# Attention weights: two of the eight diagonal chunks of a head turned by transfers, with products of their own for the last 128 columns

## The chip, the cores and the metric

The kernel runs on one core of one Trainium2 chip. The metric is the device time of one execution in microseconds, taken as the median over several executions; a profile of one execution shows where the time is spent. The engines are TensorE (PE in the profile, its weight loads PEld), VectorE (DVE), ScalarE (ACT), GpSimd (POOL) and SyncE (SP), whose queue issues nearly all transfers.

## The reference, cut to what matters

The program is a two-layer decoder trunk over 1024 positions with width 1024: a recurrent layer with a feed-forward network, then a stick-breaking attention layer with 16 heads of 64 dimensions and another feed-forward network. The change concerns the attention alone, which the reference computes in blocks of 128 rows:

```python
z = jnp.einsum("bhqd,bhkd->bhqk", qb, kb).astype(jnp.float32) * scale
strict = s_idx < t_idx
log_fail = jnp.where(strict, jax.nn.log_sigmoid(-z), 0.0)
suffix = lax.cumsum(log_fail, axis=3, reverse=True) - log_fail
weights = jnp.where(strict, jnp.exp(jax.nn.log_sigmoid(z) + suffix), 0.0)
outs.append(jnp.einsum("bhqk,bhkd->bhqd", weights.astype(vb.dtype), vb))
```

A weight is a difference of two neighbouring running products of sigmoids along the row, taken from the diagonal backwards. The kernel therefore computes the running products themselves and multiplies them with differences of neighbouring values of v, so that no weight is ever formed.

## The kernel before, in words

A head's rows are eight blocks j of 128 (0 to 7), its keys two halves of 512. `chunk_list` gives twelve chunks a head: eight diagonal ones (block j against the half that holds its diagonal, as wide as needed; those of blocks 3 and 7 are 512 wide) and four off-diagonal ones (blocks 4 to 7 against the first half, each 512 wide). For a chunk, `z_part` multiplies q and k on TensorE (L1680, L1681), `z_rest` takes the sigmoid on ScalarE (L1693) into a tile `w`, and `scan` runs the product along the row on VectorE (L1700 for diagonal chunks, L1703 for the others, which start from the first column of the diagonal chunk of the same row block).

The products with v need the chunk turned, with keys on the partitions, and split into a high and a low half of 16 bits. There are two ways:

- Off-diagonal chunks go through `turn_weights`: ScalarE casts to `wx` (L1710), VectorE subtracts to get the low half (L1711), and one transfer that transposes (L1714, on SP's queue) writes both halves into tile `wt`.
- Diagonal chunks go through `t_part` and `t_split`: TensorE transposes each 128 x 128 block with the identity into PSUM (L1725), ScalarE casts to `th` (L1734), VectorE subtracts into `tl` (L1735).

`unit_list` gives twelve units a head, one for each block kb of 128 keys against a group G of four row blocks. Units 0 to 3 (G = 0) and 4 to 7 (G = 1) are diagonal; their widths are 512, 384, 256 and 128 columns, since earlier rows don't see later keys. Units 8 to 11 take the off-diagonal weights. `av_part` multiplies each unit (L1748), once with the high and once with the low half, with the same stationary operand `VV`, and sums all units of a group in one PSUM tile; the last unit evacuates it (L1759, L1760).

The order on all engines is written out by hand in one loop over steps u, one chunk and one unit a step, with the chunks ten steps ahead of the units (eleven to thirteen near the end, by `gains`). In each step the projections of a later pair of heads (`fill`, products `qk_ps` at L143 to L145) fill TensorE. In an even step the transposes and splits are made for the two units two steps ahead, then the chunk of the step before is turned by `turn`, then the new chunk is scanned. In an odd step the new chunk is scanned before the turning.

Near the end `back` is a list of loads that bring parked attention outputs back (`vh`, `vl`, `xg` from `odh` and `odl`, L1870), one or two a step on SP's queue; `out_fill` uses them for the first output products (`ob`) from step `last_two` − 5 on.

```python
some = chunks[c : c + 1]
...
now, turning = turning, [a for a in some if not a[-1]]
...
two = {x: t_part(*units[x]) for x in (u + 2, u + 3) if x % 12 < 8}
```

Of the kernel before, what the change touches and what calls it, by code (L numbers as in the profile page):

```python
# [8 lines left out]
F32 = mybir.dt.float32  # L9
F32R = mybir.dt.float32r  # L10
BF16 = mybir.dt.bfloat16
F16 = mybir.dt.float16
# [22 lines left out]
def trunk(  # L35
# [1452 lines left out]
    with ExitStack() as st:  # L1488
# [198 lines left out]

        def z_rest(ps, q, hx, j, ci, c0, c1, diag):
            n = min(c1, (j + 1) * P) - c0
            tag = f"w{j}" if diag else "w"  # L1690
            F = ap.tile([P, n], F32, tag=tag, name=tag, bufs=1 if diag else 3)
            W[q, hx, j, ci] = F
            nc.scalar.activation(F, ps[:, 0:n], AF.Sigmoid, scale=rs[:, j : j + 1])  # L1693

# [9 lines left out]

        T = {}

        def turn_weights(q, hx, j, ci, c0, c1, diag):
            F = W[q, hx, j, ci].rearrange("p (b c) -> p b c", c=P)
            wx = ap.tile([P, 4, 2, P], F16, tag="wx", name="wx", bufs=4)
            nc.scalar.copy(wx[:, :, 0], F)  # L1710
            nc.vector.tensor_sub(wx[:, :, 1], F, wx[:, :, 0])  # L1711
            if j == 4:
                T[q, hx] = ap.tile([P, 8, 4, P], F16, tag="wt", name="wt", bufs=2)
            nc.sync.dma_start(T[q, hx][:, :, j % 4], wx.rearrange("p b h c -> p (b h c)"), transpose=True)  # L1714
# [5 lines left out]
        def t_part(q, hx, G, kb, first, last):  # L1720
            j0 = max(kb, 4 * G)
            tp = psT.tile([P, NB], F32, tag="T", name="wt_ps")
            for j in range(j0, 4 * G + 4):
                c = (j - 4 * G) * P
                nc.tensor.transpose(  # L1725
                    tp[:, c : c + P], W[q, hx, j, kb // 4][:, (kb % 4) * P : (kb % 4 + 1) * P], ident
                )
            return tp

        def t_split(tp, q, hx, G, kb, first, last):  # L1730
            q0 = (max(kb, 4 * G) - 4 * G) * P
            th = ap.tile([P, NB], F16, tag="th", name="th", bufs=3)
            tl = ap.tile([P, NB], F16, tag="tl", name="tl", bufs=3)
            nc.scalar.copy(th[:, q0:], tp[:, q0:])  # L1734
            nc.vector.tensor_sub(tl[:, q0:], tp[:, q0:], th[:, q0:])  # L1735
            return th, tl

        av, oo = {}, {}
# [1 line left out]
        def av_part(tht, q, hx, G, kb, first, last):  # L1740
            q0 = (max(kb, 4 * G) - 4 * G) * P
            if first:
                av[0] = psO.tile([P, NB], F32, tag="o", name="av_ps")
            ps = av[0]
            if tht is None:
                tht = [T[q, hx][:, 2 * kb + x].rearrange("p j c -> p (j c)") for x in range(2)]
            for x, t in enumerate(tht):
                nc.tensor.matmul(  # L1748
                    ps[:, q0:], lhsT=VV[q][:, hx, kb], rhs=t[:, q0:], start=first and x == 0, stop=last and x == 1
                )  # L1750
            if not last:
                return
            a, b = (top, bot)[:: 1 if hx == 0 else -1]

            def gather():
                if hx == 0:
                    oo[q, G] = ap.tile([P, NB], F32, tag="oo", name="oo", bufs=2)
                o = oo[q, G]
                nc.scalar.copy(o[a], ps[b])  # L1759
                nc.vector.tensor_add(o[a], ps[a], o[a])  # L1760

            def add_v():
                eng = nc.vector if q >= NP - 2 else nc.gpsimd
                eng.tensor_add(oo[q, G], oo[q, G], VT[q][:, G * NB + 1 : (G + 1) * NB + 1])

            def parts():
                o = oo[q, G]
                down = f32(av_[q])

                def both(hi, lo):  # L1770
                    nc.scalar.activation(hi, o, AF.Copy, scale=down)
                    nc.vector.scalar_tensor_tensor(lo, o, down, f32(hi), op0=ALU.mult, op1=ALU.subtract)

                if not kept(q, G):
                    both(xh[q][G], xl[q][G])
                else:
                    oh = ap.tile([P, NB], F32R, tag="oh", name="oh", bufs=1)
                    both(oh, o.bitcast(F32R))

                    def store():  # L1780
                        nc.sync.dma_start(od[q, G][0], f32(oh))
                        nc.sync.dma_start(od[q, G][1], o)

                    stage(store)

            later.insert(0, gather)
            if hx == 1:
                later.extend((add_v, lambda: None, parts))
# [32 lines left out]
        with tc.manual_schedule(engines={E.PE, E.Activation, E.DVE, E.Pool, E.SP}):  # L1821


            load_link(1)
            first = qkv_steps(0)
            between = {
                12: lambda: stats(rbc[0], psO, "o", 0),
                16: lambda: stats(rbc[1], psO, "o", 1),
                17: lambda: broadcast_r(psO, "o", 0),
                18: lambda: nc.gpsimd.tensor_scalar_mul(rs, rcol, -SC),  # L1830
                21: lambda: broadcast_r(psO, "o", 1),
            }
            def due():
                now = soon[:]
                soon.clear()
                for steps, task in now:
                    if steps > 1:
                        stage(task, steps - 1)
                    else:
                        task()  # L1840

            for i in range(1, 2 * ND * NH + 3 + AHEAD):
                next(first)
                if i in between:
                    between[i]()
                due()
                if i > 4 and later:
                    later.pop(0)()

            gains = [len(units) - x for x in (31, 29, 27)]  # L1850

            last_two, out_work = len(units) - 2 * 12, out_fill()
            amount = {x: 2 for x in (9, 10, 11, 12)}
            amount.update({x: 1 for x in (*range(-5, 1), *range(14, 21))})
            c = 0

            def turn(some):
                for a in some:
                    turn_weights(*a)

            for u in range(-LEAD, len(units)):
                some = chunks[c : c + 1]
                c += 1
                if u < -2:
                    for _ in range(2):
                        next(fill, None)
                due()
                for _ in range(2 if u >= last_two - 8 and u % 2 == 0 else 1):
                    if back:
                        nc.sync.dma_start(*back.pop(0))  # L1870
                for a in some:
                    z_rest(z_part(*a), *a)
                    if u % 2 or u < -2:
                        scan(*a)
                now, turning = turning, [a for a in some if not a[-1]]
                if u % 2 or u < -2:
                    turn(now)
                if u % 2 == 0 and u >= 0:
                    av_part(ready.pop(u, None), *units[u])
                if u % 2 == 0 and 0 <= u + 2 < len(units):  # L1880
                    two = {x: t_part(*units[x]) for x in (u + 2, u + 3) if x % 12 < 8}
                    for x, tp in two.items():
                        ready[x] = t_split(tp, *units[x])
                if u % 2 == 0 and u >= -2:
                    turn(now)
                    for a in some:
                        scan(*a)
                if u - last_two == 9:
                    mix[0].w[mix[0].order[1]] = next_weights(mix[0].raw.pop(1), nc.gpsimd)
                if later:  # L1890
                    later.pop(0)()
                if u >= -2:
                    for _ in range(2):
                        next(fill, None)
                for _ in range(amount.get(u - last_two, 0)):
                    next(out_work)
                if u in gains:
                    z_rest(z_part(*chunks[c]), *chunks[c])
                    scan(*chunks[c])
                    if not chunks[c][-1]:  # L1900
                        turning.append(chunks[c])
                    c += 1
                if u % 2 and u >= 0:
                    av_part(ready.pop(u, None), *units[u])
            while later or soon:
                due()
                if later:
                    later.pop(0)()
# [46 lines left out]
```

## Time and profile before

| | |
|---|---|
| time, median of 3 runs | 2152.64 us (2151.5 to 2154.63) |
| profiled execution: time | 2151.32 us |
| profiled execution: span | 2149.3 us, granted TensorE clock 0.998 |
| attention stage | about 985 to 1430 us of the span |
| transposes of weights on TensorE (L1725) | 320 |
| transfers that turn weights (L1714) | 64 |
| products with v (L1748) | 384 |

The span reaches from the first to the last instruction; the time holds some 2 us around it. A busy share is an average over the whole span, so a stage is judged by the busy times of its own stretches. For TensorE the distance between two starts is the price of a matmul, since the duration in the profile holds the passage through the array, which overlaps the next one. In a group row the numbers behind the bar are the total busy time, the mean duration in ns, and the idle time of the engine just before these instructions with what ended it.

### The profile page before, as it was taken

How to read it: one execution, taken by the hardware profiler on the slowest of the kernel's cores; microseconds unless marked ns; L12 is line 12 of the kernel's file. 1: busy time of each engine (PE TensorE's matmuls, PEld its weight loads, DVE VectorE, ACT ScalarE, POOL GpSimd, SP SyncE). 2: the span in 40 equal slices, each digit the busy share in tenths (PEclk: the TensorE clock that was granted, in tenths of full speed). 3: DMA queues.
4: the chain of work that ended last, by engine and by line, in shares of the span. 5: the costliest groups of instructions: out<-in, count | busy, mean ns of one | idle time of the engine just before them, and what ended most of it. 6: DMA issues, size and time to landing. Idle time of an engine off the chain costs nothing. (4 is left out here: it accounts for less than half of the span.)

```text
span 2149.3 us, 28075 instructions
## 1 busy us (share of the span) xinstructions
PE 2127.2 (99%) x10158; PEld 1742.8 (81%) x10158; DVE 1778.7 (83%) x2609; ACT 1136.3 (53%) x1838; POOL 129.0 (6%) x100
## 2 busy tenths in 40 slices
PE   8999999999999999999999999899999999999998
PEld 7888888888888888888777777668888888888887
DVE  7887768888888888896899899877888888888886
ACT  6567435444444545564666666544544444454556
POOL 1222020000000000000000000002000000000002
PEclk9999999999999999999999999999999999999999
DMA  7111422334445774536667677972234444586442
GB/s 236 49 50 39 155 96 64 116 111 155 138 154 169 275 231 136 161 119 145 140 149 151 153 156 157 216 235 96 70 109 127 153 133 156 187 276 227 134 155 90
DMA packets 390314, 315.45 MB, mean 147 GB/s; under 512 B 101272, under 2 KB 296992, under 8 KB 390176
## 3 DMA queue, kind: packets, MB, share of 16 engines
q1 hardware_dynamic: 390016, 313.40, 49.9%
q8 instruction: 79, 1.29, 0.2%
q14 instruction: 59, 0.48, 0.1%
q10 hardware_dynamic: 160, 0.27, 0.0%
HBM read 184.09 MB, written 83.36 MB: 124 GB/s over the span
## 5 line engine op out<-in xcount | busy, mean ns | idle before, releaser
L143 PE MATMUL p_ps<-vh,wbh 128*128 128x512 f32 x524 | 204.9, 391 | 0.0
L144 PE MATMUL p_ps<-vl,wbh 128*128 128x512 f32 x524 | 204.5, 390 | 0.0
L143 PE MATMUL p_ps<-vh,wch 128*128 128x512 f32 x524 | 204.2, 390 | 0.0
L145 PE MATMUL p_ps<-vh,wcl 128*128 128x512 f32 x524 | 204.1, 389 | 0.0
L145 PE MATMUL p_ps<-vh,wbl 128*128 128x512 f32 x524 | 203.9, 389 | 0.0
L144 PE MATMUL p_ps<-vl,wch 128*128 128x512 f32 x524 | 203.9, 389 | 0.0
L722 ACT CAST wbh<-sb 128x1024 fp32r<-128x1024 f32 (+2 forms) x69 | 69.6, 1009 | 191.6 <-DVE sb L702 191.6
L1693 ACT ACTIVATE w<-z_ps,rs 128x128 f32<-128x128 f32 (+1 forms) x192 | 110.9, 580 | 100.1 <-PE z_ps L1681 99.8
L145 PE MATMUL p_ps<-vh,wal 128*128 128x512 f32 x396 | 154.0, 389 | 0.0
L143 PE MATMUL p_ps<-vh,wah 128*128 128x512 f32 x396 | 154.0, 389 | 0.0
L144 PE MATMUL p_ps<-vl,wah 128*128 128x512 f32 x396 | 154.0, 389 | 0.0
L1700 DVE TENSOR_TENSOR_SCAN w<-w,unit 128x128 f32<-128x128 f32 (+3 forms) x128 | 104.9, 830 | 17.4 <-ACT w L1693 17.1
L145 PEld LDWEIGHTS p_ps<-vh,wbl 128*128 128x128 f32 x524 | 98.4, 188 | 21.1
L145 PEld LDWEIGHTS p_ps<-vh,wcl 128*128 128x128 f32 x524 | 98.4, 188 | 21.0 <-DVE wcl L736 0.6
L144 PEld LDWEIGHTS p_ps<-vl,wch 128*128 128x128 f32 x524 | 98.4, 188 | 20.5
L143 PEld LDWEIGHTS p_ps<-vh,wch 128*128 128x128 f32 x524 | 98.3, 188 | 20.5 <-ACT tb L1181 0.2
L143 PEld LDWEIGHTS p_ps<-vh,wbh 128*128 128x128 f32 x524 | 98.6, 188 | 19.7 <-ACT U L1181 0.4
L144 PEld LDWEIGHTS p_ps<-vl,wbh 128*128 128x128 f32 x524 | 98.6, 188 | 18.5
L143 PE MATMUL qk_ps<-vh,whi 128*128 128x512 f32 x264 | 111.9, 424 | 0.0
L145 PE MATMUL qk_ps<-vh,wlo 128*128 128x512 f32 x264 | 103.6, 392 | 0.0
L144 PE MATMUL qk_ps<-vl,whi 128*128 128x512 f32 x264 | 103.3, 391 | 0.0
L143 PE MATMUL p_ps<-vh,wd 128*128 128x512 f32 x254 | 99.4, 391 | 0.1
(402 smaller groups left out, 5796.3 us busy)
## 6 DMA issues: line engine op xcount, KB each, us to landing
raw<-in_ffn_w_in SPq DMA_DIRECT2D x88, 512.0 KB, 4.1
vl<-pd SPq DMA_DIRECT2D x128, 256.0 KB, 3.5
pd<-U SPq DMA_DIRECT2D x90, 256.0 KB, 2.3
kk<-two SPq DMA_DIRECT2D x64, 256.0 KB, 4.5
raw<-in_ffn_w_out SPq DMA_DIRECT2D x56, 256.0 KB, 3.6
raw<-in_attn_w_qkv SPq DMA_DIRECT2D x24, 512.0 KB, 5.4
h<-hd SPq DMA_DIRECT2D x32, 256.0 KB, 5.4
hd<-h SPq DMA_DIRECT2D x32, 256.0 KB, 2.0
```

Of the source, the lines that this page charges most:

```text
L143: nc.tensor.matmul(ps, lhsT=wh, rhs=mh, start=first, stop=False, **kw)
L144: nc.tensor.matmul(ps, lhsT=wh, rhs=ml, start=False, stop=False, **kw)
L145: nc.tensor.matmul(ps, lhsT=wl, rhs=mh, start=False, stop=last, **kw)
L722: nc.scalar.copy(self.full(self.wb), self.full(self.sb))
L1693: nc.scalar.activation(F, ps[:, 0:n], AF.Sigmoid, scale=rs[:, j : j + 1])
L1700: nc.vector.tensor_tensor_scan(rev, rev, unit[:, NB - n :][:, ::-1], 0.0, op0=ALU.mult, op1=ALU.add)
```

## The change

The diagonal chunks of row blocks 3 and 7, two a head, go the way of the off-diagonal chunks: cast and subtraction into `wx`, then a transposing transfer into a new tile `wd`. The last 128 columns of each diagonal unit (row block 3 or 7) are taken from `wd`, in two products of their own; what is left for `t_part` and `t_split` are 384, 256 and 128 columns for the first three units of a group and nothing for the fourth. The weights of block 3 now use the shared tile `w` with three buffers, as nothing but the transfer reads them; block 7 keeps its own, whose first column the off-diagonal scan reads.

```diff
         def z_rest(ps, q, hx, j, ci, c0, c1, diag):
             n = min(c1, (j + 1) * P) - c0
-            tag = f"w{j}" if diag else "w"
-            F = ap.tile([P, n], F32, tag=tag, name=tag, bufs=1 if diag else 3)
+            tag = f"w{j}" if diag and j != 3 else "w"
+            F = ap.tile([P, n], F32, tag=tag, name=tag, bufs=1 if tag != "w" else 3)
...
+        def by_transfer(q, hx, j, ci, c0, c1, diag):
+            return not diag or j % 4 == 3
+
         def turn_weights(q, hx, j, ci, c0, c1, diag):
...
+            if diag:
+                T[q, hx, j] = ap.tile([P, 8, P], F16, tag="wd", name="wd", bufs=2)
+                nc.sync.dma_start(T[q, hx, j], wx.rearrange("p b h c -> p (b h c)"), transpose=True)
+                return
...
-            for j in range(j0, 4 * G + 4):
+            for j in range(j0, 4 * G + 3):
...
-            th = ap.tile([P, NB], F16, tag="th", name="th", bufs=3)
-            tl = ap.tile([P, NB], F16, tag="tl", name="tl", bufs=3)
-            nc.scalar.copy(th[:, q0:], tp[:, q0:])
-            nc.vector.tensor_sub(tl[:, q0:], tp[:, q0:], th[:, q0:])
+            th = ap.tile([P, NB - P], F16, tag="th", name="th", bufs=3)
+            tl = ap.tile([P, NB - P], F16, tag="tl", name="tl", bufs=3)
+            nc.scalar.copy(th[:, q0:], tp[:, q0 : NB - P])
+            nc.vector.tensor_sub(tl[:, q0:], tp[:, q0 : NB - P], th[:, q0:])
...
-            if tht is None:
-                tht = [T[q, hx][:, 2 * kb + x].rearrange("p j c -> p (j c)") for x in range(2)]
-            for x, t in enumerate(tht):
+            if kb // 4 != G:
+                turned = [T[q, hx][:, 2 * kb + x].rearrange("p j c -> p (j c)") for x in range(2)]
+                parts_ = [(0, NB, t, 0) for t in turned]
+            else:
+                parts_ = [(NB - P, NB, T[q, hx, 4 * G + 3][:, 2 * (kb % 4) + x], 0) for x in range(2)]
+                if tht is not None:
+                    parts_ = [(q0, NB - P, t, q0) for t in tht] + parts_
+            for i, (c0, c1, t, t0) in enumerate(parts_):
                 nc.tensor.matmul(
-                    ps[:, q0:], lhsT=VV[q][:, hx, kb], rhs=t[:, q0:], start=first and x == 0, stop=last and x == 1
+                    ps[:, c0:c1], lhsT=VV[q][:, hx, kb], rhs=t[:, t0 : t0 + c1 - c0],
+                    start=first and i == 0, stop=last and i == len(parts_) - 1,
                 )
...
-                now, turning = turning, [a for a in some if not a[-1]]
+                now, turning = turning, [a for a in some if by_transfer(*a)]
...
-                    two = {x: t_part(*units[x]) for x in (u + 2, u + 3) if x % 12 < 8}
+                    two = {x: t_part(*units[x]) for x in (u + 2, u + 3) if x % 12 < 8 and x % 4 < 3}
...
-                    if not chunks[c][-1]:
+                    if by_transfer(*chunks[c]):
```

Three places show how the order of instructions moves. The first is TensorE in a middle head, at the first unit of the second group (`th`, `tl` and `wd` are the turned weights, `v` the stationary operand, `ident` the identity of the transposes, `qk` the filling projection). Before:

```order
L1681 MATMUL z_ps<-kk,q 128x512
L1748 LDWEIGHTS v
L1748 MATMUL av_ps<-th,v 128x512
L1748 LDWEIGHTS v
L1748 MATMUL av_ps<-tl,v 128x512
L1725 MATMUL wt_ps<-ident,w_8796 128x128
L1725 MATMUL wt_ps<-ident,w_8828 128x128 x2
L143 MATMUL qk_ps<-vh_2_2550,whi 128x512
```

With the change:

```order
L1681 MATMUL z_ps<-kk,q 128x512
L1760 LDWEIGHTS v
L1760 MATMUL av_ps<-th,v 128x384
L1760 LDWEIGHTS v
L1760 MATMUL av_ps<-tl,v 128x384
L1760 LDWEIGHTS v
L1760 MATMUL av_ps<-wd,v 128x128
L1760 LDWEIGHTS v
L1760 MATMUL av_ps<-wd,v 128x128
L1732 MATMUL wt_ps<-ident,w_8805 128x128
L143 MATMUL qk_ps<-vh_2_2550,whi 128x512
```

Two products became four over the same 512 columns, and of three transposes for the units two steps ahead one is left.

The second place is VectorE in a later head, from the splits of the first two units (L1735, then L1742) over the off-diagonal scans (L1703) to the splits of the next two. Before:

```order
L1735 TENSOR_TENSOR tl<-wt_ps,th 128x512
L1735 TENSOR_TENSOR tl<-wt_ps,th 128x384
L1703 SCALAR_TENSOR_TENSOR w<-w,w_9469 128x512
L1559 TENSOR_TENSOR wlo<-raw,whi 128x512
L1703 SCALAR_TENSOR_TENSOR w<-w,w_9484 128x512
L1711 TENSOR_TENSOR wx<-w,wx 128x4x128
L1735 TENSOR_TENSOR tl<-wt_ps,th 128x256
L1735 TENSOR_TENSOR tl<-wt_ps,th 128x128
L1711 TENSOR_TENSOR wx<-w,wx 128x4x128
```

With the change:

```order
L1742 TENSOR_TENSOR tl<-wt_ps,th 128x384
L1742 TENSOR_TENSOR tl<-wt_ps,th 128x256
L1714 TENSOR_TENSOR wx<-w_9546,wx 128x4x128
L1703 SCALAR_TENSOR_TENSOR w<-w,w_9483 128x512
L1559 TENSOR_TENSOR wlo<-raw,whi 128x512
L1703 SCALAR_TENSOR_TENSOR w<-w,w_9505 128x512
L1714 TENSOR_TENSOR wx<-w,wx 128x4x128
L1742 TENSOR_TENSOR tl<-wt_ps,th 128x128
L1714 TENSOR_TENSOR wx<-w,wx 128x4x128
```

The subtraction for block 7 (from `w_9546`) stands between the splits and the first off-diagonal scan, and the splits are narrower and one fewer.

The third place is SP's queue near the end of the stage, where the first loads of `back` begin (`raw` is a weight load, `kk` spreads the keys). Before:

```order
L116 DMA raw<-in_attn_w_o 128x8x128 x2
L1714 DMA_TRANSPOSE wt<-wx 128x8x128
L1642 DMA kk<-two 64x2x512 x4
L1714 DMA_TRANSPOSE wt<-wx 128x8x128 x2
L1870 DMA vh_3_2532<-odh_0_7885 128x512
L1714 DMA_TRANSPOSE wt<-wx 128x8x128
L1870 DMA vl_3_2533<-odl_0_7886 128x512
```

With the change:

```order
L116 DMA raw<-in_attn_w_o 128x8x128 x2
L1717 DMA_TRANSPOSE wd<-wx 128x8x128
L1721 DMA_TRANSPOSE wt<-wx 128x8x128
L1642 DMA kk<-two 64x2x512 x4
L1721 DMA_TRANSPOSE wt<-wx 128x8x128 x2
L1883 DMA vh_3_2532<-odh_0_7885 128x512
L1721 DMA_TRANSPOSE wt<-wx 128x8x128
L1883 DMA vl_3_2533<-odl_0_7886 128x512
```

One `wd` transfer stands ahead of the four `wt` transfers of the head; four more (two for each of the last two heads) stand among and behind the loads that follow.

## The prediction

> **What bounds the kernel now.** I read the head of the page, then the busy times of long stretches of the attention stage, then TensorE's timeline inside a steady head, and last the waits at the end of the stage.
>
> ```profile
> span 2149.3 us, 28075 instructions
> PE 2127.2 (99%) x10158; PEld 1742.8 (81%) x10158; DVE 1778.7 (83%) x2609; ACT 1136.3 (53%) x1838; POOL 129.0 (6%) x100
> ```
>
> The kernel is one long stream on TensorE. The attention stage runs from about 985 to 1430 us; its stretches (columns: stretch, length, busy PE, PEld, DVE, ACT, POOL, granted clock, DMA share, GB/s) say whether that holds there too:
>
> ```profile
> 1180.00:1280.00 100.00, 100.00 (x526) 75.82 (x525) 89.65 (x137) 62.18 (x122) 7.74 (x9) 1.00 0.74 160
> 1280.00:1380.00 100.00, 98.28 (x519) 74.33 (x517) 90.79 (x137) 64.08 (x126) 8.77 (x9) 1.00 0.76 164
> 1380.00:1440.00 60.00, 51.59 (x240) 35.58 (x241) 46.66 (x66) 32.55 (x60) 3.03 (x2) 0.94 0.88 252
> ```
>
> In the steady part TensorE is busy without a gap at full clock, so each ns less of TensorE work is a ns of time. VectorE is 90% busy, near enough to matter. In the last 60 us TensorE waits 8.4 us, and the transfers are at 0.88: there TensorE is not the only bound. The change must be costed in these two places apart.
>
> **TensorE, per group of four diagonal units.** A matmul's price is the distance between starts; the second column holds its passage too and is not summed.
>
> ```profile
> 1203.39 0.34 PE L1748 MATMUL av_ps<-th,v 128*128 128x384 f16 x1
> 1203.57 0.33 PE L1748 MATMUL av_ps<-tl,v 128*128 128x384 f16 x1
> 1203.60 0.41 PE L1680 MATMUL z_ps<-kk,q 128*128 128x256 f32 x1
> 1203.85 0.28 PE L1681 MATMUL z_ps<-kk,q 128*128 128x256 f32 x1
> 1203.97 0.28 PE L1748 MATMUL av_ps<-th,v 128*128 128x256 f16 x1
> 1204.09 0.27 PE L1748 MATMUL av_ps<-tl,v 128*128 128x256 f16 x1
> 1204.20 0.93 PE L1725 MATMUL wt_ps<-ident,w 128*128 128x128 f32 x7
> 1204.88 0.47 PE L143 MATMUL qk_ps<-vh,whi 128*128 128x512 f32 x1
> 1205.19 0.39 PE L144 MATMUL qk_ps<-vl,whi 128*128 128x512 f32 x1
> ...
> 1207.97 0.23 PE L1748 MATMUL av_ps<-th,v 128*128 128x128 f16 x1
> 1208.04 0.22 PE L1748 MATMUL av_ps<-tl,v 128*128 128x128 f16 x1
> 1208.07 0.42 PE L1680 MATMUL z_ps<-kk,q 128*128 128x384 f32 x1
> 1208.33 0.34 PE L1681 MATMUL z_ps<-kk,q 128*128 128x384 f32 x1
> 1208.51 0.39 PE L1748 MATMUL av_ps<-th,v 128*128 128x512 f16 x1
> 1208.73 0.38 PE L1748 MATMUL av_ps<-tl,v 128*128 128x512 f16 x1
> 1208.95 0.49 PE L1725 MATMUL wt_ps<-ident,w 128*128 128x128 f32 x3
> 1209.20 0.47 PE L143 MATMUL qk_ps<-vh,whi 128*128 128x512 f32 x1
> 1209.51 0.39 PE L144 MATMUL qk_ps<-vl,whi 128*128 128x512 f32 x1
> ```
>
> *Removed.* A 512-column product by itself takes 0.22 (1208.51 to 1208.73). Seven transposes with the product behind them take 1205.19 − 1204.20 = 0.99, so 0.77 without it; three take 1209.51 − 1208.95 = 0.56, so 0.34. One transpose is worth (0.77 − 0.34)/4 = 0.1075 us. A group goes from 7 + 3 to 5 + 1 transposes, four fewer: **−0.43 us**.
>
> *Added.* The columns streamed stay the same, but eight products become fourteen. A 128-column pair takes 0.07 for its first (1207.97 to 1208.04), and to the second z product 0.36; less the 0.18 of a 384-column z product (1208.33 to 1208.51) the pair costs 0.18, of which the second product takes 0.11: the f32 weight load behind it isn't covered by so short a stream. Pairs of 256, 384 and 512 columns cost 0.23 (1203.97 to 1204.20), 0.34 (1203.39 to 1203.85 less 0.12 of z) and 0.44. Now unit 0 is 0.34 + 0.18 = 0.52 for 0.44, unit 1 is 0.23 + 0.18 = 0.41 for 0.34, unit 2 is two pairs of 128, 0.18 + 2 × 0.07 = 0.32 for 0.23, and unit 3 is one such pair as before. **+0.24 us**; net −0.19 per group.
>
> Two groups a head, sixteen heads: 32 groups. Thirteen heads run before the first wait at the end of the stage; the wide products of the thirteenth start here:
>
> ```profile
> 1354.28 0.61 PE L1748 MATMUL av_ps<-wt,v 128*128 128x512 f16 x2
> ```
>
> So 26 groups × 0.19 = **4.9 us** fully on the path, and 6 × 0.19 = 1.1 us where TensorE waits anyway; I count half, **0.6 us**.
>
> Bounds: a transpose at 0.083 (three start within 0.25) leaves 0.33 removed; and should a short product behind another cost a whole weight load (99 ns by its group, below) instead of 0.07, five of them add 5 × 0.03 = 0.15. Both: +0.06 a group, a loss of 1.6 us over 26. The other end is a short product at its bare stream, 0.23/4 = 0.06, for 0.24 saved a group, 6.2 us. I keep 0.19, since the 0.07 is the spacing of exactly such a pair.
>
> The Trainium skill, page "TensorE: Matmul & The Clock Gate", section "Back-to-back issue gap", states about 81 ns for each 128-column product in a stream that loads weights for each, which speaks against splitting products; the pair above shows 70 ns. By the page five products cost 0.055 more, the group saves 0.135, the 26 groups 3.5 us, and the sum below would be 2150.5.
>
> **VectorE and ScalarE.**
>
> ```profile
> L1711 DVE TENSOR_TENSOR wx<-w,wx 128x512 f16<-128x512 f32 x64 | 48.3, 756 | 2.8 <-ACT wx L1710 2.1
> L1710 ACT CAST wx<-w 128x512 f16<-128x512 f32 x64 | 39.9, 625 | 16.0 <-DVE w L1703 7.9 <-issue 6.1 <-ACT w L1693 1.1
> L1748 PEld LDWEIGHTS <-v 128*128 128x128 f16 x384 | 22.8, 99 | 43.3 <-issue 38.7 <-DVE tl L1735 1.0 <-DMA xg<-odl 0.5
> L1735 DVE TENSOR_TENSOR tl<-wt_ps,th 128x512 f16<-128x512 f32 x32 | 21.9, 686 | 19.1 <-ACT th L1734 19.1
> L1734 ACT CAST th<-wt_ps 128x512 f16<-128x512 f32 x32 | 18.7, 586 | 7.4 <-PE wt_ps L1725 6.8
> L1735 DVE TENSOR_TENSOR tl<-wt_ps,th 128x256 f16<-128x256 f32 x32 | 13.5, 420 | 6.5 <-ACT th L1734 5.6
> ```
>
> The splits of a group were 512, 384, 256 and 128 wide and become 384, 256 and 128, so the 512 one is lost: 586 ns on ScalarE and 686 on VectorE. In its place stand one wx copy (625) and one wx subtraction (756): +0.04 and +0.07 us a group. I cost both at nothing in the steady part, hidden behind TensorE's stream: VectorE idles 10% of it. Without that cover it is 32 × 0.07 = 2.2 us. What moves matters more: block 7's wx subtraction now stands between a pair of splits and the scans of the same head. That pair is 686 − 420 = 0.27 shorter, so the scan behind is 0.76 − 0.27 = 0.49 late, and with it the subtractions and transfers that follow.
>
> **Transfers.** One transfer that stood alone ran within 1227 to 1231; then come the last off-diagonal transfer of an odd head (the ninth), its first use, and the time from issue to landing:
>
> ```profile
> 1227.00:1231.00 4.00, 4.00 (x22) 3.07 (x20) 3.60 (x7) 3.68 (x8) 0.00 (x0) 1.00 0.39 76
> ...
> 1238.87 1.81 SPq L1714 DMA_TRANSPOSE wt<-wx  x1
> ...
> 1244.21 0.61 PE L1748 MATMUL av_ps<-wt,v 128*128 128x512 f16 x2
> ...
> DMA to landing us min/median/max: 3.0/3.4/5.9
> ```
>
> It took 0.39 × 4 = 1.56 us of all sixteen engines. There are 32 more, 50 us over some 440: the share of 0.74 goes to about 0.85. A diagonal transfer is issued six steps of the loop ahead of its first product; a head has twelve steps and takes (1354.28 − 1244.21)/4 = 27.5 us, so 13.8 us stand against the 3.4. That hides it. Its buffer was last read three steps (6.9 us) before, except in the last head, where the read stands in the same step, so SP waits there for the product with the loads behind it. The off-diagonal transfers have less room: 1238.87 + 3.4 = 1242.3 against 1244.2, 1.9 us. Late by 0.49 they still arrive.
>
> **The end of the stage.** Here loads that bring kept products back share SP's queue with the transfers:
>
> ```profile
> 1375.46 1.26 SPq L1714 DMA_TRANSPOSE wt<-wx  x1
> 1376.77 0.57 SPq L1870 DMA_DIRECT2D vl<-odl  x1
> ...
> 1380.92 0.51 PE L144 MATMUL ob<-vl,whi 128*128 128x512 f32 x1 [2.43 <-DMA vl<-odl]
> ...
> 1382.00:1384.00 2.00, 2.00 (x7) 0.85 (x6) 1.75 (x3) 1.88 (x5) 0.00 (x0) 0.50 0.93 278
> 1384.00:1386.00 2.00, 1.97 (x7) 1.12 (x5) 2.00 (x4) 0.66 (x1) 0.00 (x0) 0.83 0.92 259
> ...
> 1393.52 0.49 PE L143 MATMUL ob<-vh,whi 128*128 128x512 f32 x1 [2.40 <-DMA vh<-odh]
> ```
>
> The first load stands behind the last off-diagonal transfer of the fourteenth head, which waits for its subtraction: 0.49 us later. The second stands behind one more diagonal transfer with the engines at 0.92: 1.56 us later. Together **+2.0 us**, between nothing and the 10 us of the second rival.
>
> **Sum.** 2151.3 (the profiled execution's time) − 4.9 − 0.6 + 2.0 = 2147.8. The median of the runs, 2152.64, lies 1.3 above it: **2149.1 us**.
>
> **Rivals.**
> *The whole saving.* The waits at the end don't grow, since the transfers find SP idle: −4.9 − 1.1 = −6.0, **2146.6**. Speaking for it is that each diagonal transfer has at least six steps; against it that the engines are at 0.88.
> *The end gets late (slower).* Three diagonal transfers stand in or ahead of the queue of loads, 3 × 1.56 = 4.7 us, and their subtractions on a saturated VectorE add 3 × 0.756 = 2.3. After the first wait the clock stood at 0.50 and 0.83 for two stretches of 2 us, 1.0 + 0.3 = 1.3 us lost; two further gaps of that size cost 2.6. Together 9.6 less 4.9: +4.7, **2157.3**. It decides from the point where the loads are pushed by about 5 us; before that the saving outweighs it. The same page of the Trainium skill, section "Part 1: The HAM clock gate", puts the halved clock behind an idle window of about 3.4 us; here a wait of 2.43 was enough, so the trace is stricter.
> *Off-diagonal transfers late in odd heads.* If a diagonal transfer's 1.56, its 1.26 on SP (1375.46 above) and the 0.49 all add up, 3.3 exceeds the 1.9 of room by 1.4 us; the seven odd heads among the first thirteen give 9.8 − 3.5 = +6.3, **2158.9**. Speaking for it is the small room; against it that SP stands idle in between.
> *Short products at a whole weight load.* +1.6 + 2.0 on the median: **2156.2**, with the bound above.
>
> **How the numbers follow.** The forecast has 0.45 (2147 to 2152), the whole saving 0.22, the late end 0.15, the late transfers 0.12, the weight load 0.06. What this measurement can tell from no change is about 0.2%, 4.3 us: below 2148.3 or above 2156.9. Faster: 0.20 of the whole saving and 0.12 of the forecast, 0.32. Slower: 0.10 of the late end, 0.08 of the late transfers, 0.02 of the last, 0.20. Within: 0.48. The range runs from 2145.4 (6.2 and 1.1 saved with no wait) to 2157.5, between the late end and the late transfers.
>
> **What would show it.** Right: transposes on TensorE at 192 instead of 320, spacings of 0.07 and 0.11 in the wd products, TensorE 100% busy in the steady part with a head about 0.38 us shorter (27.1), and the two waits for loads a little longer than 2.4. Wrong: TensorE waiting for wt or wd in the steady part, VectorE full there, or a third wait for a load. If the short products show spacings near 0.1, the saving is gone.

## The result, and the profile after

The changed kernel takes 2142.41 us, the median of six runs (2141.65 to 2144.23), against 2152.07 for the kernel before in six runs (2150.78 to 2154.63). The ratio is 0.9954, with a 95% interval of 0.9944 to 0.9964. That is 9.7 us faster. The forecast was 2149.1, some 3.5 us faster on the median shown then, and its range reached down to 2145.4. The direction was right, and the size lies outside the range.

First the head of the page after, then a stretch of the steady part (columns as in the prediction):

```profile
span 2140.0 us, 28244 instructions
PE 2116.5 (99%) x10222; PEld 1735.1 (81%) x10222; DVE 1778.7 (83%) x2609; ACT 1137.5 (53%) x1838; POOL 125.8 (6%) x100
```

```profile
1180.00:1280.00 100.00, 100.00 (x554) 76.26 (x554) 91.88 (x137) 65.86 (x128) 8.14 (x10) 1.00 0.90 178
```

The span fell by 9.3 us (from 2149.3). TensorE is still busy without a gap from 1180 to 1280, now with the transfers at 0.90 where they stood at 0.74, and VectorE at 92% where it was at 90%. So the time was not found in a wait that went away: the stream itself is shorter.

Where it became shorter is seen by the starts of the heads, that is of each head's first `wt` products. The ninth and the thirteenth head, in the timeline of TensorE after:

```profile
1237.59 0.61 PE L1760 MATMUL av_ps<-wt,v 128*128 128x512 f16 x2
...
1344.91 0.61 PE L1760 MATMUL av_ps<-wt,v 128*128 128x512 f16 x2
```

The four heads between take (1344.91 − 1237.59)/4 = 26.83 us, where before they took 27.52. All twelve steps from the first to the thirteenth head are equally 0.69 us shorter, which is 0.34 us a group; the forecast had 0.19 a group, 0.38 a head. The thirteenth head starts 9.37 us earlier than before (1354.28), and the program ends 9.3 us earlier: behind the thirteenth head nothing more is gained or lost.

TensorE in a middle head after, first unit 0 of the second group, then unit 1, the z products and unit 2 of a first group:

```profile
1220.62 0.34 PE L1760 MATMUL av_ps<-th,v 128*128 128x384 f16 x1
...
1220.96 0.28 PE L1760 MATMUL av_ps<-wd,v 128*128 128x128 f16 x2
1221.07 0.28 PE L1732 MATMUL wt_ps<-ident,w 128*128 128x128 f32 x1
...
1221.42 0.39 PE L144 MATMUL qk_ps<-vl,whi 128*128 128x512 f32 x1
...
1224.41 0.28 PE L1760 MATMUL av_ps<-th,v 128*128 128x256 f16 x1
...
1224.64 0.27 PE L1760 MATMUL av_ps<-wd,v 128*128 128x128 f16 x2
1224.73 0.36 PE L1680 MATMUL z_ps<-kk,q 128*128 128x256 f32 x1
1224.93 0.28 PE L1681 MATMUL z_ps<-kk,q 128*128 128x256 f32 x1
1225.05 0.23 PE L1760 MATMUL av_ps<-th,v 128*128 128x128 f16 x1
...
1225.17 0.28 PE L1760 MATMUL av_ps<-wd,v 128*128 128x128 f16 x2
1225.28 0.72 PE L1732 MATMUL wt_ps<-ident,w 128*128 128x128 f32 x5
...
1226.06 0.39 PE L144 MATMUL qk_ps<-vl,whi 128*128 128x512 f32 x1
```

These rows are to be laid beside the prediction's from before, from the first product to the second of the filling projection. Unit 0 with its transposes took 1209.51 − 1208.51 = 1.00 and takes 1221.42 − 1220.62 = 0.80: −0.20, where the forecast's prices give +0.08 − 0.215 = −0.135. Units 1 and 2 with their transposes took 1205.19 − 1203.39 = 1.80 and take 1226.06 − 1224.41 = 1.65: −0.15, against +0.16 − 0.215 = −0.055.

The price that was wrong stands in the `wd` rows. A pair of 128 columns takes 0.11 where transposes follow (1220.96 to 1221.07, and 1225.17 to 1225.28), two pairs in a row 0.23 (1225.05 to 1225.28). Only where an f32 product follows does the pair cost what the forecast put everywhere: from 1224.64 to the second z product are 0.29, less the 0.12 of a 256-column z product 0.17. The groups of weight loads after differ with it (columns: busy us and mean ns of one, then the idle time ahead of them):

```profile
L1732 PEld LDWEIGHTS wt_ps<-ident,w 128*128 128x128 f32 x192 | 22.7, 141 | 3.0
L143 PEld LDWEIGHTS p_ps<-vh,wch 128*128 128x128 f32 x524 | 98.3, 188 | 20.5 <-ACT tb L1181 0.2
```

The load of a transpose takes 141 ns, that of an f32 product 188. That the short pair covers the one and not the other to its end would account for the two prices, but the records do not show it; the two prices themselves are in the spacings.

One unit 2 in each head, that of the second group, has no transposes behind it but an f32 product. After, with unit 1 ahead of it, and then the same place before:

```profile
1233.15 0.28 PE L1760 MATMUL av_ps<-th,v 128*128 128x256 f16 x1
...
1234.30 0.39 PE L144 MATMUL qk_ps<-vl,whi 128*128 128x512 f32 x1
```

```profile
1212.51 0.34 PE L1748 MATMUL av_ps<-th,v 128*128 128x384 f16 x1
...
1213.54 0.39 PE L144 MATMUL qk_ps<-vl,whi 128*128 128x512 f32 x1
```

There nothing is taken away and 1.15 − 1.03 = 0.12 is added; the forecast had 0.16, a third more. With the five transposes of the next head that stand behind the `wt` products (two fewer, −0.21), a head sums to −0.20 − 0.15 − 0.20 + 0.12 − 0.21 = −0.64, which leaves 0.05 of the measured 0.69 to the rounding of five differences of rows.

**The end of the stage**, from the thirteenth head's first `wt` product to the last one, after and before:

```profile
1344.91:1419.47 74.56, 64.21 (x336) 44.38 (x336) 61.88 (x91) 42.52 (x83) 4.60 (x5) 0.93 1.03 244
```

```profile
1354.28:1429.33 75.05, 64.92 (x325) 44.69 (x324) 61.54 (x91) 42.82 (x84) 4.74 (x5) 0.95 0.91 233
```

This piece holds six groups, 6 × 0.34 = 2.1 us less work, and is only 0.5 us shorter, so 1.6 us are paid back there. TensorE's waits in the two pieces, what it waited for, us in total, times, longest, after and then before:

```profile
PE ob L143 <- DMA vh<-odh: 4.2, 3, 1.7
PE z_ps L1680 <- ACT w L1693: 2.5, 3, 1.9
PE ob L144 <- DMA vl<-odl: 1.4, 3, 1.0
PE ob L144 <- DMA xg<-odl: 1.1, 1, 1.1
PE av_ps L1760 <- DVE tl L1742: 0.9, 2, 0.5
PE av_ps L1760 <- ACT th L1741: 0.3, 1, 0.3
```

```profile
PE ob L144 <- DMA vl<-odl: 2.7, 2, 2.4
PE ob L143 <- DMA vh<-odh: 2.7, 2, 2.4
PE av_ps L1748 <- DVE tl L1735: 2.2, 4, 0.8
PE av_ps L1748 <- ACT th L1734: 2.2, 2, 1.7
```

The waits for loads rose from 5.4 to 6.7 us, those for ScalarE's `w` by 2.3 (0.2 before), and those for the narrower splits fell from 4.4 to 1.2: together 10.4 against 10.0 with that 0.2, almost the same. The rest is the clock: 0.93 against 0.95 of about 75 us, near 1.4 us at this rounding; TensorE's busy time agrees, as it fell by 64.92 − 64.21 = 0.7 us where 2.1 us of work went. After, the halved clock lasts longer in one place, behind the first long wait there:

```profile
1370.00:1372.00 2.00, 1.04 (x2) 0.53 (x3) 2.00 (x5) 1.43 (x3) 0.00 (x0) 0.50 0.87 224
1372.00:1374.00 2.00, 2.00 (x7) 1.28 (x7) 2.00 (x3) 0.98 (x3) 0.00 (x0) 0.50 0.74 155
1374.00:1376.00 2.00, 2.00 (x5) 1.04 (x5) 1.52 (x3) 1.39 (x3) 0.00 (x0) 0.50 0.91 291
```

This account of the end is read from two executions and was not tested by a run of its own, such as one that turns the last two heads' chunks on TensorE again. Two runs below bear on it. From the thirteenth head's first `wt` product to the last instruction the profiled executions took 795.0 us before and 795.1 with the change. Experiment 1, which keeps the change's transfers and puts the transposes back, took 795.2: so behind the thirteenth head neither the transfers nor TensorE's saving shows in the time. And experiment 8c, whose work is that of the change, took 796.8, so the parts of 1 to 2 us above are no larger than what one execution differs from another.

### The profile page after: what moved, and what is told of

The parts are those of the page before. It is cut to its first block, busy times and chain, and to the rows that moved or that the text cites. A ratio compares the mean times of both kernels' runs of the same rounds, so it can differ in the third digit from the quotient of the medians.

```text
span 2140.0 us, 28244 instructions
## 1 busy us (share of the span) xinstructions
PE 2116.5 (99%) x10222; PEld 1735.1 (81%) x10222; DVE 1778.7 (83%) x2609; ACT 1137.5 (53%) x1838; POOL 125.8 (6%) x100
## 4 chain that ended last, share of the span: by engine, by line
PE 96%; DVE 2%; DMA 1%; ACT 1%; issue 1%; SPq 0%; DVEq 0%; ACTq 0%
PE p_ps L143 18%; PE p_ps L145 18%; PE p_ps L144 18%; PE qk_ps L143 4%; PE qk_ps L145 4%; PE qk_ps L144 4%; PE av_ps L1760 3%; PE a_ps L144 3%; PE a_ps L145 3%; PE a_ps L143 3%; PE ob_ps L145 3%; PE ob_ps L143 3%; PE ob_ps L144 3%; PE z_ps L1680 2%; PE z_ps L1681 2%; PE i_ps L145 1%
```

## The experiments

All ran beside the kernel before, whose median was 2152.5 to 2152.8 in them. "A head" is always the mean of the twelve steps from the first to the thirteenth head's first `wt` product, 27.52 us before and 26.83 with the change. Experiment 2 is made from the kernel before, all others from the change. The theory after the result was that the transposes are worth what the prediction said, and that the split products cost less than half of its price, by what follows them.

**1. The transposes put back.** The four transposes a group that the change takes away are run again, into columns of the same tile that nobody reads; all else is the change.

```diff
+            r = kb % 4
+            for c in (NB - P, 0)[: 1 + (r == 2)]:
+                nc.tensor.transpose(tp[:, c : c + P], W[q, hx, 4 * G + 2, kb // 4][:, r * P : (r + 1) * P], ident)
```

> The changed kernel with the four transposes a group put back on TensorE (128 in all, of another block, into columns that nothing reads); all else as in the change. Theory (a transpose is worth 0.1075 us, and the surplus of the result over the prediction lies in the price of the short products): a steady head, 26.83 us with the change, takes 8 x 0.1075 = 0.86 us more, 27.69, and the time is about 12 us above the change, some 2154. Rival (the short products do cost 0.24 a group as predicted, and a transpose is worth (0.343 + 0.24)/4 = 0.146): a head takes 1.17 more, 28.00, and the time is about 16 us above the change, some 2158.

Measured: 2154.57 us, ratio 1.0008 (0.9999 to 1.0018); a head 27.76. The eight transposes of a head cost 27.76 − 26.83 = 0.93 us, 0.116 each: the prediction's 0.1075 was a little low. (The twelfth step alone is 0.18 longer than its like; without it a transpose costs 0.114.) The rival, by which the products cost what the prediction said and the transposes were worth (0.343 + 0.24)/4 = 0.146, falls: it asks for a head of 28.0.

**2. The split alone.** The kernel before, with only the products cut in two at column 384; the same columns of the same tiles, so nothing else moves.

```diff
-            for x, t in enumerate(tht):
+            cuts = [(q0, NB)] if kb // 4 != G else [(q0, NB - P), (NB - P, NB)][q0 == NB - P :]
+            parts_ = [(c0, c1, t) for c0, c1 in cuts for t in tht]
+            for i, (c0, c1, t) in enumerate(parts_):
                 nc.tensor.matmul(
-                    ps[:, q0:], lhsT=VV[q][:, hx, kb], rhs=t[:, q0:], start=first and x == 0, stop=last and x == 1
+                    ps[:, c0:c1], lhsT=VV[q][:, hx, kb], rhs=t[:, c0:c1],
+                    start=first and i == 0, stop=last and i == len(parts_) - 1,
                 )
```

> The kernel before with only the products split: the last 128 columns of each diagonal unit are multiplied in two products of their own, from the same th and tl. No transfer is added, no transpose removed. Theory (a pair of 128 costs its bare stream where a transpose or another 16-bit product follows, and 0.07 more only where an f32 product follows): unit 1 of both groups 0.07, unit 2 of the second group 0.06, unit 0 0.015: 0.23 us a head, 27.52 becomes 27.75, the time about +3.5 us on the kernel before. Rival (the prediction: 0.24 a group wherever it stands): 0.48 a head, 28.0, the time about +7.5 us.

Measured: 2154.63 us, ratio 1.0011 (1.0001 to 1.0020); a head 27.74, 0.22 us longer than before. The prediction's price was 2 × 0.24 = 0.48 a head. Unit 0 in TensorE's timeline of this kernel:

```profile
1210.66 0.34 PE L1750 MATMUL av_ps<-th,v 128*128 128x384 f16 x1
...
1211.00 0.22 PE L1750 MATMUL av_ps<-th,v 128*128 128x128 f16 x1
1211.05 0.22 PE L1750 MATMUL av_ps<-tl,v 128*128 128x128 f16 x1
1211.11 0.50 PE L1725 MATMUL wt_ps<-ident,w 128*128 128x128 f32 x3
```

From 1210.66 to 1211.11 the unit takes 0.45, where the uncut pair of 512 took 0.44 before (1208.51 to 1208.95): ahead of transposes the cut is nearly free. Unit 1, which an f32 product follows, in the same timeline, from its first product to the second z product:

```profile
1205.45 0.28 PE L1750 MATMUL av_ps<-th,v 128*128 128x256 f16 x1
...
1205.97 0.28 PE L1681 MATMUL z_ps<-kk,q 128*128 128x256 f32 x1
```

It takes 0.52, where it took 0.46 before the cut (1203.39 to 1203.85). Read in the same way, the cut costs 0.01 in each unit 0, 0.08 in units 1 and 2 of the first group together and 0.12 in those of the second, whose unit 2 has an f32 product behind it too. That is the 0.22 of a head, and nearly all of it stands ahead of f32 products. The two experiments add up: −0.93 + 0.22 = −0.71, against −0.69 for the whole change. With that the steady part is accounted for.

**3. The short pair first, in unit 1.** The `wd` products of unit 1 stand ahead of its wide ones, so that a 256-column product and not a short one is followed by the f32 z product.

```diff
-                    parts_ = [(q0, NB - P, t, q0) for t in tht] + parts_
+                    wide = [(q0, NB - P, t, q0) for t in tht]
+                    parts_ = parts_ + wide if kb % 4 == 1 else wide + parts_
```

> The changed kernel with the order turned in unit 1 of each group alone: the two wd products come before the two wide ones, so that a 256-column stream stands ahead of the f32 product. Theory (the 0.07 is the f32 weight load behind a stream that is too short for it): 0.07 a group less, a head 26.83 becomes 26.69, the time about 2 us below the change, 2140. Rival (the price sits in the short products themselves, whatever follows): no change, 26.83 and 2142.

Measured: 2141.51 us, ratio 0.9945 (0.9930 to 0.9960); a head 26.72, −0.11. TensorE's timeline of it:

```profile
1224.44 0.28 PE L1761 MATMUL av_ps<-wd,v 128*128 128x128 f16 x2
1224.56 0.27 PE L1761 MATMUL av_ps<-th,v 128*128 128x256 f16 x1
1224.67 0.27 PE L1761 MATMUL av_ps<-tl,v 128*128 128x256 f16 x1
1224.70 0.36 PE L1680 MATMUL z_ps<-kk,q 128*128 128x256 f32 x1
1224.90 0.28 PE L1681 MATMUL z_ps<-kk,q 128*128 128x256 f32 x1
```

From the first of the unit to the second z product are 0.46; with the change 0.52 (1224.41 to 1224.93). The same products in another order cost 0.06 less: this part of the price belongs to the neighbour, not to the short product. It is three quarters of what was expected (0.11 of 0.14 a head). The gain in the total is within the intervals.

**4. Unit 3's pair moved up behind unit 2's.** The last place where a short pair stands ahead of f32 products, in both groups, on top of experiment 3.

```diff
+                    if u % 12 in (2, 6):
+                        av_part(None, *units[u + 1])
...
-                if u % 2 and u >= 0:
+                if u % 2 and u >= 0 and u % 12 not in (3, 7):
```

> As the run before (wd first in unit 1), and the two wd products of unit 3 moved one step up, right behind those of unit 2, where transposes or one f32 product follow, so that one f32 product fewer stands behind a short one in each group. Theory: a further 0.065 a group less, a head 26.56, the time about 4 us below the change, 2138. Rival: no change against the change, or a loss at the end of the stage where the first group's sum is evacuated a step earlier.

Measured: 2139.40 us, ratio 0.9937 (0.9922 to 0.9952); a head 26.69, only −0.03 beyond experiment 3. The expectation was missed for the mean, and not through the price. In the rows a move gains 0.07: six products in a row cost 0.11 more than four, and the place that they left saves 0.18. Every second head is accordingly 0.15 shorter than in experiment 3 (26.43 against 26.58), a little more than was expected. But the heads between them got a wait of 0.24 us that was not there:

```profile
1206.55 0.23 PE L1761 MATMUL av_ps<-th,v 128*128 128x128 f16 x1
1206.86 0.22 PE L1761 MATMUL av_ps<-tl,v 128*128 128x128 f16 x1
```

These starts are 0.31 apart instead of 0.06: `tl` was late. With the pair moved the sums of a row block are finished a step earlier, and VectorE's evacuation of them came ahead of the split. Right behind it, while GpSimd worked on the evacuated sums, a subtraction for the filling projection took 1.52 us, where it took 0.66 in experiment 3. A rearrangement on TensorE alone moved VectorE's work.

**5. The transposes ahead of the products.** In even steps the transposes are issued before the products, so that an f32 product follows every last pair.

```diff
-                if u % 2 == 0 and u >= 0:
-                    av_part(ready.pop(u, None), *units[u])
...
+                if u % 2 == 0 and u >= 0:
+                    av_part(ready.pop(u, None), *units[u])
+                for x, tp in two.items():
+                    ready[x] = t_split(tp, *units[x])
```

> The changed kernel with one order turned: in an even step the transposes for later units come ahead of the step's products with v, so that the short wd products are followed by an f32 product instead of a transpose (three places a head: unit 2 of the first group and unit 0 of both). Nothing is added or left out. Theory (a short product costs 0.06 to 0.07 more exactly where an f32 product stands behind it): about 0.2 us a head more, 26.83 becomes 27.0, the time about 3 us above the change, 2145. Rival (what stands behind it is of no matter, and unit 1 in the second group of runs gained for another reason): 26.83 and 2142.

Measured: 2142.91 us, ratio 0.9955 (0.9938 to 0.9972); a head 26.94. Two of the twelve steps are longer than their like, by 0.37 and 0.24 us. They end where an off-diagonal transfer landed late, once with a wait that the profile shows:

```profile
1185.73 0.59 PE L1760 MATMUL av_ps<-wt,v 128*128 128x512 f16 x2 [0.21 <-DMA wt<-wx]
```

The undisturbed steps average 26.89, +0.06, a third of what was expected. The direction holds and the size doesn't: the pair does cost 0.17 in the rows where it had cost 0.11, but half of it comes back at the front, where a transpose and no longer an f32 product stands ahead of the 16-bit ones: there 0.02 to 0.03 are saved. What an order costs is seen only with both neighbours.

**6. Each diagonal transfer issued twice**, to the same tile, to see how far the transfers are from deciding.

```diff
-                nc.sync.dma_start(T[q, hx, j], wx.rearrange("p b h c -> p (b h c)"), transpose=True)
+                for _ in range(2):
+                    nc.sync.dma_start(T[q, hx, j], wx.rearrange("p b h c -> p (b h c)"), transpose=True)
```

> The changed kernel with each of the 32 diagonal transfers issued twice, the second writing the same data to the same tile; all else as in the change. Theory (the transfers are hidden in the steady part, with 0.88 of the transfer engines busy there and 6 us of SP's time to spare a head): the steady heads stay at 26.83 although the share goes to about 1.0, and the cost comes at the end of the stage alone, some 2 to 6 us. Rival (the transfers are already at their limit, and the change's gain hangs on the little that is left): the off-diagonal transfers come late in every second head and the heads grow by 0.5 us or more, over 6 us in all and more at the end.

Measured: 2202.39 us, ratio 1.0232 (1.0212 to 1.0253); a head 29.74. These are the rival's numbers, but not for its reason. Waits of SP and of TensorE in this kernel:

```profile
SPq L1718 <- DMA wd<-wx: 77.9, 32, 5.2
```

```profile
PE av_ps L1761 <- DMA wt<-wx: 17.7, 9, 3.4
```

SP waited each of 32 times for the first transfer to land before it issued the second into the same tile, 77.9 us in all, and the `wt` transfers queued behind it came late. The sixteen engines were no fuller than with the change (0.87 from 1023 to 1344 in both). So it tells what a stop on SP's queue costs, and nothing about room on the engines; experiment 8 was made for that.

**7. Each diagonal subtraction done twice** on VectorE (the second writes the same values).

```diff
-            nc.vector.tensor_sub(wx[:, :, 1], F, wx[:, :, 0])
+            for _ in range(2 if diag else 1):
+                nc.vector.tensor_sub(wx[:, :, 1], F, wx[:, :, 0])
```

> The changed kernel with the VectorE subtraction of the diagonal chunks done twice (32 more of about 0.7 us, two a head, same result); all else as in the change. Theory (VectorE idles 8% of a steady head, about 2.1 us, so 1.4 more are still hidden): steady heads stay at 26.83, and only the end of the stage is later, by 1 to 3 us. Rival (VectorE sets the pace in places of a head already): heads grow by up to 1.4 us, some 18 us in all.

Measured: 2146.84 us, ratio 0.9973 (0.9962 to 0.9983); a head 27.02. The twelve heads of this kernel:

```profile
1023.00:1344.00 321.00, 319.72 (x1757) 243.12 (x1757) 305.90 (x463) 204.73 (x402) 25.26 (x30) 1.00 0.84 173
```

VectorE rose to 305.90 of 321 us, 95% (92% with the change), and TensorE fell short of full by 1.3 us. Most heads took 26.9, two took 27.5 and 27.7: in the one `tl` was late (a wait of 0.4 us), in the other an off-diagonal transfer (0.8). So the cover held for most of a second copy of the work, and frayed at 95%. In the profiled execution, which at 2150.01 us is 3.2 above the median, the heads lose 12 × 0.19 = 2.3 us, and some 3.5 more are lost behind the thirteenth.

**8. A spare transfer**, of three quarters of the size, into a tile that nobody reads, behind each diagonal transfer. To make room for the tile, `th` and `tl` have two buffers instead of three.

```diff
+                spare = ap.tile([P, 6, P], F16, tag="spare", name="spare", bufs=1)
+                nc.sync.dma_start(spare, wx[:, 0:3].rearrange("p b h c -> p (b h c)"), transpose=True)
...
-            th = ap.tile([P, NB - P], F16, tag="th", name="th", bufs=3)
-            tl = ap.tile([P, NB - P], F16, tag="tl", name="tl", bufs=3)
+            th = ap.tile([P, NB - P], F16, tag="th", name="th", bufs=2)
+            tl = ap.tile([P, NB - P], F16, tag="tl", name="tl", bufs=2)
```

> The changed kernel with one more transposing transfer behind each of the 32 diagonal ones, of three quarters of its size, into a spare tile that nothing reads, so that (other than in the run that issued each transfer twice into one tile) SP need not wait for the first to land; th and tl have two buffers instead of three to make room. Theory (the 60 us of that run came from SP, which stood 78 us waiting for the first transfer of each pair; the engines themselves have room from 0.87): the steady heads stay near 26.83, at most 0.3 more, and the time is within 10 us of the change. Rival (the transfer engines are at their limit at 0.87): the heads grow by over 1 us as in that run, and the time by 20 us or more.

Measured: 2146.64 us, ratio 0.9971 (0.9961 to 0.9981); a head 26.87. The twelve heads, and the largest wait at the end:

```profile
1023.00:1344.00 321.00, 320.60 (x1770) 244.62 (x1770) 294.36 (x440) 209.73 (x405) 27.34 (x30) 1.00 0.94 190
```

```profile
PE ob L143 <- DMA vh<-odh: 7.1, 2, 4.4
```

With the transfers at 0.94 of the sixteen engines the heads are as long as with the change but for one of 27.24, at whose end TensorE waited 0.4 us for an off-diagonal transfer. The 4 us lost lie at the end of the stage, where the loads wait behind the transfers (7.1 us for `vh`, 4.2 with the change). This is the mechanism of the prediction's slower rival, seen at a dose that the change doesn't reach.

**8c. The two buffers alone**, as a control.

```diff
-            th = ap.tile([P, NB - P], F16, tag="th", name="th", bufs=3)
-            tl = ap.tile([P, NB - P], F16, tag="tl", name="tl", bufs=3)
+            th = ap.tile([P, NB - P], F16, tag="th", name="th", bufs=2)
+            tl = ap.tile([P, NB - P], F16, tag="tl", name="tl", bufs=2)
```

> The changed kernel with two buffers instead of three for th and tl and nothing else: the control of the run before. Both theories: steady heads at 26.83 and the time of the change, 2142, since a unit's th and tl are read before the unit after next is split.

Measured: 2140.90 us, ratio 0.9953 (0.9938 to 0.9967); a head 26.83. The fewer buffers cost nothing, so experiment 8 stands for the transfers alone.

**9. Experiments 3 and 4 where they pay**: the pair first in unit 1, and unit 3's pair moved up in the second group alone, where no transposes follow.

```diff
+                    if u % 12 == 6:
+                        av_part(None, *units[u + 1])
...
-                if u % 2 and u >= 0:
+                if u % 2 and u >= 0 and u % 12 != 7:
```

> wd first in unit 1 of both groups, and unit 3's two wd products moved up behind those of unit 2 in the second group alone, so that the first group's sum is evacuated where it was. Theory (the run that moved both lost 0.24 us in every second head where VectorE's split came late behind the earlier evacuation, and gained 0.05 a move otherwise): heads at 26.58 to 26.68, no head with the 0.24, the time some 2.5 us below the change, 2139.5. Rival (the move itself brings nothing): 26.72 as with wd first alone, and 2141.

Measured: 2139.44 us, ratio 0.9943 (0.9930 to 0.9957); a head 26.65, the shortest of all, and without the 0.24 us waits of experiment 4. Its median is 3 us below the change's, and the intervals of the two ratios overlap, so a gain over the change in the total is likely and not established; the 0.18 us a head is seen in the trace, 12 times over.

## Why the prediction was wrong

**The short products were mis-sized.** This is the term that failed: "unit 0 is 0.34 + 0.18 = 0.52 for 0.44 […] +0.24 us" a group. The measured cost is 0.22 a head, 0.11 a group (experiment 2), since the 0.18 had been read off a pair with a z product behind it and was then put also on unit 0 and on the unit 2 with transposes behind it. The rows to see it by stood in the prediction's own fence: it noted that the 0.18 came from "the f32 weight load behind", and didn't ask which load stands behind the pair elsewhere. Its bound "0.06, for 0.24 saved a group" wasn't one, as it made only the first product of a pair cheaper and left the second at 0.11; 0.34 lies beyond it. The forecast was too high at every place, most where transposes follow (0.08 for a unit 0 that cost 0.01). It had 4.9 us over 26 groups, and 26 × 0.343 = 8.9 were measured: 4.0 us of the miss.

**The transposes** were right: 0.1075 forecast, 0.116 by experiment 1.

**The end of the stage** was put at +2.0 − 0.6, so 1.4 us of net loss, and nothing was lost on balance (9.37 us ahead at the thirteenth head, 9.3 at the end). The parts differ from the forecast's. The waits for loads did grow, by 1.3 us instead of 2.0; waits for ScalarE came and waits for splits went, which it had not foreseen; and the longer dip of the clock ate most of the six groups' own saving, of which it had counted half. Each of these is read from one execution and no larger than their scatter, so that no cost is seen at the end, and why is not settled. This is 1.4 of the miss; 0.4 us more stood already at the start of the stage, where the kernels of the experiments differ by up to 2 us, and isn't put down to the change. The last 0.9 is the distance of the median from the profiled execution: 1.3 in the forecast, 0.4 measured (2142.41 against 2142.03).

**VectorE and ScalarE at nothing in the steady part** was right, with TensorE full. VectorE's 90% became 92%, and experiment 7 shows the cover fraying at 95%. **The transfers hidden** was right too, but with less room than was read. The share forecast at 0.85 came to 0.90, no wait for `wt` or `wd` appeared in the thirteen heads, and at 0.94 one did in twelve heads (experiment 8). The room of 1.9 us for the off-diagonal transfers had been worked out with the median of 3.4 us to landing. The very transfer that it was read for, issued at 1238.87, landed after 4.7 us, so it had 0.6 us of room; its like after, issued at 1232.29, landed after 4.9 and had 0.4 until 1237.59. A delay of half a microsecond is thus about what these transfers bear, and the forecast of no wait came true with some luck.

**The rivals.** The whole saving (2146.6) came nearest, its waits at the end about as before; but it too saved less than was measured, having the same price of the short products in it. The late end did not happen at this dose. Late off-diagonal transfers did not either, though they were nearer than the prediction thought: experiments 5, 7 and 8 have one or two each, and experiment 6 has nine, by waits on SP's queue that the change doesn't have. Short products at a whole weight load: the spacing behind another short product is 0.05 to 0.07 us and not 0.1. The 81 ns of the Trainium skill's page "TensorE: Matmul & The Clock Gate", section "Back-to-back issue gap", are not borne out by these rows either.

## What to carry to other kernels

The price of a short product is made by its neighbours: read it from a row with the same instruction behind it, and when an edit puts it in several places, price each place by what follows there. Look at an order within a step with the same eyes: moving a short pair away from an f32 product (experiments 3 and 9) is worth 0.05 to 0.07 us a place for nothing. A bound is one only if every term that shares the doubt is moved to its end together.

## What the runs showed of the hardware

The granted clock went to 0.50 with a wait of 1.74 us (the product after it starts at 1369.89) and stood there for three stretches of 2 us, where before, behind a wait of 2.43, it was one such stretch with 0.82 ahead of it and 0.83 after it. The Trainium skill, page "TensorE: Matmul & The Clock Gate", section "Part 1: The HAM clock gate", has an idle window of about 3.4 us ahead of the halved clock; both waits here are shorter, and what else lowered the clock isn't settled.

```profile
1369.89 0.80 PE L143 MATMUL ob<-vh,whi 128*128 128x512 f32 x1 [1.74 <-DMA vh<-odh]
```

Sixteen DMA engines at 0.94 still delivered all transfers in time in eleven of twelve heads, while 77.9 us of SP's waiting for its own earlier transfers cost 60 us at a share of 0.87: the queue's order mattered more than the load on the engines. And the 16-bit products of a step took 0.02 to 0.03 us less when a transpose and not an f32 z product stood ahead of them (experiment 5), which is seen by comparing two places, not in a row by itself.
